# Layer 1 of a two-layer decoder trunk: issue order held from its first stage, and the main products reordered to keys, values, receptance, gate

## Chip, cores and metric

The kernel runs on one NeuronCore of a Trainium2 chip. The metric is the device time of one execution in microseconds (us); the kernel before takes 2486.07 us, the median of three runs (2485.39 to 2491.46). A difference of 0.3% is 7.5 us.

## The reference

A sequence of 512 tokens with 2048 features passes two layers, all in float32. Layer 0 is a forgetting attention; the change does not touch its work. Layer 1 is RWKV-7 time mixing (here without the constants):

```python
h = rms_norm(x, norm_w[1]) * (1 + scale) + shift
xx = pad(h[:, :-1]) - h                       # the token before, minus this one
xr, xw, xk, xv, xa, xg = (h + xx * mu[i] for i in range(6))
r, k, v, z = xr @ w_in[0], xk @ w_in[1], xv @ w_in[2], xg @ w_in[3]
w_log = -softplus(-(w0 + tanh(xw @ w1) @ w2)) - 0.5;  decay = exp(-exp(w_log))
v = v + (v_first - v) * sigmoid(v0 + (xv @ v1) @ v2)
a = sigmoid(a0 + (xa @ a1) @ a2)
kk = normalised(k * k_k);  k = k * (1 + (a - 1) * k_a)
for t: S = S * w_t + (S @ a_t) b_t + v_t k_t;  y_t = S @ r_t      # per head of 64, a = -kk, b = kk * a
y = group_norm(y) * lnx_w + lnx_b + sum(r * k * r_k) * v
x = x + gate * ((y * silu(z)) @ w_out)
```

So the receptance r, the key k, the value v and the gate z are four products of 2048 x 2048, each from its own mix of h with the token before, and the output is a fifth. The scan over the tokens is computed in chunks of 64 tokens.

## The kernel before

Features lie on the 128 partitions, in KT = 16 tiles of 128 x 512 tokens. A product of float32 accuracy is three matmuls in float32r: weight and operand are each split into `hi` (a copy on ScalarE, ACT) and `lo` (a subtraction on VectorE, DVE), and `mm3` adds hi x hi, lo-weight x hi and hi x lo-operand in one PSUM bank. One output tile of a main product is 16 x 3 = 48 matmuls of 512 columns.

Layer 1 has these stretches.

- **First stage.** One loop over the 16 feature tiles k. It forms the normalised tile `xn` (DVE), the hidden tile `hp` (ACT, stored to `h1d`), the difference to the token before `d`, the key's mix `m` and its split, the split of one 128 x 768 slice of the key weight (`wst1`), and 18 matmuls into six banks: the first six key tiles. It also forms the mixes of the receptance and of the gate (ACT multiplies, GpSimd (POOL) adds) and stores them to `mxd[1]` and `mxd[2]`. In this loop the three compute engines are not held to program order; the scheduler of the framework may put one tile's work ahead of another's.
- **Main products.** `backbone` runs over a list of output tiles: ten remaining keys, 16 receptances, 16 values, 16 gates, 16 outputs. Their operands come from `mixed`, which loads a stored mix and splits it, when a tile of the operand before is spent. Two PSUM banks (`pj`) take turns; tile i waits in the plan until the work behind tile i - 2 has let go of its bank (`freed`). At the boundary between two products two tiles are interleaved.
- **Side work.** While `backbone` writes out its matmuls, a planner (`Flow`) interleaves generators by a planned clock `fl.t`, which counts the matmuls written so far: first `lora_k` (three small products, and the value's mix, stored to `mxd[0]`), then `lora_up`, then `keys` (one per head pair, 9.8 planned us apart) with `invert` and `inverse` (a triangular inverse, most of it on POOL, then through TensorE), then, when all 16 inverses are stored (`qd`), the pool `rk` is opened and `stage` and `chain` run the recurrence: 16 chains, each begun at least 12 hops of 2.15 planned us after the one before.
- **Order.** From `backbone` on, PE (TensorE), DVE and ACT each issue in exactly the order in which the program was written (`e.on = True`). SP (SyncE) issues nearly all transfers, on one queue.

`values` needs the pool `rk` for its buffers, which before is open only after the inverses; `stage` needs `rd` (a receptance tile stored) and `vd` (a value tile stored and transposed). `gated` waits for `yd` (a chain's output stored).

Of the kernel before, what the change touches and what calls it, by code (L numbers as in the profile page):

```python
# [9 lines left out]
F = mybir.dt.float32  # L10
# [7 lines left out]
P = 128  # L18
# [111 lines left out]
def body(ctx, tc, a, out, dbg=None, stop=0):  # L130
# [49 lines left out]
    bsc = cp.tile([P, 2, KT], F, name="bsc")  # L180
    for l in range(2):
        pool.tensor_scalar(bsc[:, l, :], vecs[:, V_BM + 3 * l + 1, :], 1.0, None, op0=OP.add)
    mraw = cp.tile([P, 6, 2 * KT], F, name="mraw")
    shift = cp.tile([P, 2, KT], F, name="shift")
    scale = cp.tile([P, 2, KT], F, name="scale")
    gate = cp.tile([P, 2, KT], F, name="gate")
# [6 lines left out]
    pool.memset(floor, 2.0 ** 26 * 1e-24 / DH)  # L193
    oka = cp.tile([P, KT], F, name="oka")
    pool.tensor_scalar(oka, vecs[:, V_KA, :], -1.0, 1.0, op0=OP.mult, op1=OP.add)
    lnb = cp.tile([P, 1], F, name="lnb")
    pool.memset(lnb, 10.0 * LN2)
    center = cp.tile([P, P], F, name="center")
# [65 lines left out]
    def mod_unit(mp, cb, l, part, t):  # L264
        for h in range(2):
            s = slice(h * D // 2, (h + 1) * D // 2)
            w = mp.tile([P, D // 2], F, tag="wm", name="wm", bufs=3)
            sp.dma_start(w, a["wmodT"][l, part * KT + t][:, s])
            yield 4.5
            dve.tensor_tensor_reduce(out=w, in0=w, in1=cb[:, s], scale=1.0, scalar=0.0,  # L270
                                     op0=OP.mult, op1=OP.add,
                                     accum_out=mraw[:, 3 * l + part, 2 * t + h:2 * t + h + 1])
            mdone.add((l, part, t, h))
        m0, m1 = (mraw[:, 3 * l + part, 2 * t + h:2 * t + h + 1] for h in range(2))
        b = vecs[:, V_BM + 3 * l + part, t:t + 1]
        if part == 1:
            b = bsc[:, l, t:t + 1]
        o = (shift, scale, gate)[part][:, l, t:t + 1]
        pool.tensor_scalar(o, m0, m1, b, op0=OP.add, op1=OP.add)
        if part == 1:  # L280
            pool.tensor_scalar(o, o, vecs[:, V_NW + l, t:t + 1], 1.0, op0=OP.mult, op1=OP.mult)
# [105 lines left out]
    with ExitStack() as s0:  # L387
# [7 lines left out]
        with tc.tile_pool(name="st0", bufs=2, reuse_waits="tile") as q:  # L395
# [201 lines left out]
        def until(i):  # L597
            while i is not None and i not in ends:
                yield 0.2
# [313 lines left out]
        backbone(fl, tiles, at, ready, ends, {n - 2, n} if 1 else ())  # L913
        fl.drain()
        gst.close()
        for e in (pe, dve, act):
            e.on = False
        ss = bank("ss")
        for i, t in enumerate(acc):
            pe.matmul(ss, onesD, t, start=i == 0, stop=i == 1)  # L920
# [8 lines left out]
        A = []  # L929
        ks = [bank(t) for t in ("pj", "pj", "x", "x", "S", "S")]  # L930
        with tc.tile_pool(name="st1", bufs=2, reuse_waits="tile") as q:
            for k in range(KT):
                xp = q.tile([P, T + 1], F, tag="xn", name="xn")
                xn = xp[:, 1:]
                pool.tensor_scalar(xp[:, 0:1], shift[:, 1, k:k + 1], -1.0, 1.0, op0=OP.mult,
                                   op1=OP.mult)
                dve.scalar_tensor_tensor(out=xn, in0=x1[k], scalar=scale[:, 1, k:k + 1],
                                         in1=rstd1, op0=OP.mult, op1=OP.mult)
                hp = q.tile([P, T + 1], F, tag="hp", name="hp")
                pool.memset(hp[:, 0:1], 0.0)  # L940
                act.activation(hp[:, 1:], xn, AF.Identity, bias=shift[:, 1, k:k + 1])
                sp.dma_start(h1d[k], hp)
                w = wload(a["wst1"][k:k + 1].rearrange("k p n -> p k n"), 1, NS1, "s", q)
                A.append(new_act(k))
                d = q.tile([P, T], F, tag="d", name="d")
                dve.tensor_tensor(out=d, in0=xp[:, 0:T], in1=xn, op=OP.subtract)
                m = q.tile([P, T], F, tag="m", name="m")
                dve.scalar_tensor_tensor(out=m, in0=d, scalar=vecs[:, V_MU + 2, k:k + 1],
                                         in1=hp[:, 1:], op0=OP.mult, op1=OP.add)
                split(A[k][0], A[k][1], m)  # L950
                for i, n in ((1, 0), (2, 5)):
                    m = q.tile([P, T], F, tag=f"m{n}", name="m")
                    act.activation(m, d, AF.Copy, scale=vecs[:, V_MU + n, k:k + 1])
                    pool.tensor_tensor(out=m, in0=m, in1=hp[:, 1:], op=OP.add)
                    sp.dma_start(mxd[i, k], m)
                for i, o in enumerate(ks):
                    mm3(o, w, 0, A[k], k == 0, k == KT - 1, i * P, (i + 1) * P)

# [8 lines left out]
    fl = Flow()  # L967
    NK = KT - len(ks)
    mq = ctx.enter_context(tc.tile_pool(name="mq", bufs=2, reuse_waits="tile"))
    pools = ExitStack()  # L970
    ctx.callback(pools.close)
    q = pools.enter_context(tc.tile_pool(name="kq", bufs=2, reuse_waits="tile"))
# [65 lines left out]
    def mixing(i, to, old):  # L1038
        for k in range(KT):
            while (i, k) not in premixed:  # L1040
                yield 0.2
            yield from take("m")
            fl.start(fl.t + 2, mixed(i, to, old, k, load(mq, mxd[i, k], "hp", bufs=NHP)))
            yield 0.1

    premixed = {(i, k) for i in (1, 2) for k in range(KT)}

    def keep(j, o):
        t = mq.tile([P, T], F, tag="z", name="kt")
# [110 lines left out]


    def values(j, o, e):
        while not vqs:
            yield 0.2
        vq = vqs[0]
        yield from take("vf")
        yield from take("sv")
        sv = load(vq, svd[j], "sv", bufs=1)
        vv = load(vq, vfT[j], "vf", bufs=2)
        yield from until(e)  # L1170
        dve.tensor_tensor(out=vv, in0=vv, in1=o, op=OP.subtract)
        yield 0.7
        dve.tensor_tensor(out=vv, in0=vv, in1=sv, op=OP.mult)
        free["sv"] += 1
        yield 0.7
        dve.tensor_tensor(out=vv, in0=vv, in1=o, op=OP.add)
        yield 3
        sp.dma_start(vvd[j], vv)
        n = yield from need("S")
        tr = bank("S")  # L1180
        for i in range(4):
            pe.transpose(tr[:, i * P:(i + 1) * P], vv[:, i * P:(i + 1) * P], ident)
        yield 1
# [6 lines left out]
        vd.add(j)  # L1190


    md = set()
# [438 lines left out]
    def side(q):  # L1632
# [35 lines left out]
        for j in range(KT):  # L1668
            if "v" in dbg:
                print("keys", j, fl.t, len(ends))  # L1670
            fl.start(fl.t, keys(kp, j))
            yield KEY
        while len(qd) < KT:
            yield 0.2
        yield 3
        pools.close()
        rk = pools.enter_context(tc.tile_pool(name="rk", bufs=1, reuse_waits="tile"))
        vqs.append(rk)
        for i in range(4):
            QP.append([rk.tile([P, HC, C], F, name=f"QP{i}{h}") for h in range(2)])  # L1680
            GP.append([rk.tile([P, HC, C], F, name=f"GP{i}{h}") for h in range(2)])
# [19 lines left out]
            fl.start(fl.t, chain(rk, j))  # L1701
            yield 0.1

    vqs = []
    fl.start(0, side(q))
    Av, Ar, Az, G = [], [], [], []
    ready = {(id(A), k) for k in range(KT)}
    at = {}
    tiles = [(a["wk1"][j], A, kept, j) for j in range(KT - NK, KT)]
    tiles += [(a["wr"][j], Ar, recept, j) for j in range(KT)]  # L1710
    tiles += [(a["wv1"][j], Av, values, j) for j in range(KT)]
    tiles += [(a["wz1"][j], Az, gated, j) for j in range(KT)]
    tiles += [(a["wo1"][j], G, output, j) for j in range(KT)]
    for e in (pe, dve, act):
# [1 line left out]
    pe.clock = fl  # L1716
    freed.clear()
    n0, n1, n2, n3 = NK, NK + KT, NK + 2 * KT, NK + 3 * KT
    for n, task in ((n0, mixing(1, Ar, A)), (n1, mixing(0, Av, Ar)), (n2, mixing(2, Az, Av)),
                    (n3, gathering())):  # L1720
        at[n - 2, 0] = [task]
    backbone(fl, tiles, at, ready, ends, {n - i for n in (n0, n1, n2, n3) for i in (0, 2)}, 14)
# [22 lines left out]
```

## Time and profile before

| what | number |
|---|---|
| time, median of three runs | 2486.07 us |
| the profiled execution | 2484.87 us, its span 2483.2 us |
| mean granted TensorE clock | 0.979 |
| PE busy | 2342.1 us (94%) |
| DVE, ACT, POOL busy | 1658.1, 1242.7, 756.2 us |
| DMA, mean | 192 GB/s, 476.06 MB |

Matmuls overlap, so PE's busy time is the time in which at least one runs. A timeline row gives start, duration, engine, line, operation, output<-inputs. A window row gives its length, the busy time of PE, of the weight loads, of DVE, ACT and POOL with instruction counts, the granted clock, the mean share of the 16 DMA engines that was busy, and GB/s. All instructions are issued through one helper, so they carry one line number, and tiles are told apart by name.

### The profile page before, as it was taken

The numbers are of one execution on the slowest core, as the hardware profiler recorded it, in microseconds if no ns is written. First come the engines' busy times: TensorE is split into PE (matmuls) and PEld (weight loads), VectorE is DVE, ScalarE is ACT, GpSimd is POOL, SyncE is SP. The second block draws the span as 40 slices with busy tenths as digits, with TensorE's granted clock in tenths as the row PEclk, the third lists the DMA queues.
The fourth block names the chain that finished last, engine by engine and source line by source line (L and its number), as shares of the span: only waits on it lengthen the run. The fifth ranks groups of instructions, "written<-read, shape, count | busy, mean of one in ns | idle before, by whom it ended". The sixth has DMA issues, their size and how long they took to land. (4 is left out here: it accounts for less than half of the span.)

```text
span 2483.2 us, 39895 instructions
## 1 busy us (share of the span) xinstructions
PE 2342.1 (94%) x13626; PEld 1812.4 (73%) x13626; DVE 1658.1 (67%) x3114; ACT 1242.7 (50%) x2281; POOL 756.2 (30%) x1199
## 2 busy tenths in 40 slices
PE   7998999999999999987999998887999999999999
PEld 4786677787777888865766776765777767777787
DVE  7878787888887553349796666572577876776332
ACT  3426655555556552226447676642344545555321
POOL 0003424433332200117340248720434444441000
PEclk8999999999999999999999999998999999999999
DMA  8856566666664275436657886776656656554453
GB/s 315 314 210 208 179 198 215 208 211 202 211 202 153 94 234 173 146 117 215 193 168 254 264 253 213 215 209 188 199 156 174 194 155 180 158 146 154 142 148 98
DMA packets 339260, 476.06 MB, mean 192 GB/s; under 512 B 146288, under 2 KB 156656, under 8 KB 335216
## 3 DMA queue, kind: packets, MB, share of 16 engines
q1 hardware_dynamic: 337392, 470.88, 60.5%
q0 software_dynamic: 1664, 2.63, 0.3%
q8 instruction: 108, 1.77, 0.3%
q14 instruction: 96, 0.79, 0.1%
HBM read 377.42 MB, written 95.95 MB: 191 GB/s over the span
## 5 line engine op out<-in xcount | busy, mean ns | idle before, releaser
L88 PE MATMUL pj<-hi,whi 128*128 128x512 f32 x2416 | 990.4, 410 | 16.8 <-ACT hi L88 10.3
L88 PE MATMUL pj<-hi,wlo 128*128 128x512 f32 x2416 | 954.7, 395 | 17.8 <-DVE wlo L88 17.8
L88 PE MATMUL pj<-lo,whi 128*128 128x512 f32 x2416 | 956.4, 396 | 2.3 <-DVE lo L88 2.3
L88 DVE TENSOR_TENSOR wlo<-raw,whi 128x512 fp32r<-128x512 f32 (+2 forms) x628 | 477.8, 768 | 278.5 <-ACT whi L88 276.0
L88 ACT ACTIVATE whi<-raw 128x512 fp32r<-128x512 f32 (+2 forms) x628 | 393.6, 634 | 412.6 <-PE pj L88 232.7
L88 PEld LDWEIGHTS pj<-hi,whi 128*128 128x128 f32 x2416 | 458.5, 190 | 122.7 <-ACT hi L88 11.6
L88 PEld LDWEIGHTS pj<-hi,wlo 128*128 128x128 f32 x2416 | 459.1, 190 | 108.3 <-DVE wlo L88 22.9
L88 PEld LDWEIGHTS pj<-lo,whi 128*128 128x128 f32 x2416 | 457.2, 189 | 104.1 <-DVE lo L88 3.4
L88 POOL TENSOR_SCALAR SV<-SV,dec 64x64 f32<-64x64 f32 x224 | 91.8, 410 | 221.7 <-DVE SV L88 207.3
L88 DVE CUSTOM_DVE_ANT_0 wm<-wm,cb 128x1024 f32<-128x1024 f32 x128 | 157.8, 1233 | 0.3
L88 ACT ACTIVATE pr<-Sm,mx 128x128 f32<-128x128 f32 (+3 forms) x128 | 71.5, 559 | 87.9 <-POOL mx L88 87.7
L88 POOL TENSOR_SCALAR mx<-mx 128x1 f32<-128x1 f32 x128 | 64.9, 507 | 158.2 <-DVE mx L88 110.0
L88 POOL TENSOR_SCALAR pr<-pr,rc 128x128 f32<-128x128 f32 (+3 forms) x128 | 96.0, 750 | 28.2 <-DVE rc L88 20.2
L88 DVE COPY SV<-x 64x64 f32<-64x64 f32 x256 | 56.6, 221 | 63.3 <-PE x L88 56.2
L88 DVE CUSTOM_DVE_ANT_0 Sm<-S,cmask 128x128 f32<-128x128 f32 (+3 forms) x128 | 62.1, 485 | 35.5 <-PE S L88 34.8
L88 POOL TENSOR_TENSOR lt<-lane 128x30 f32<-128x30 f32 (+14 forms) x90 | 61.3, 682 | 64.6 <-DMA lane<-mld 57.8
L88 DVE TENSOR_TENSOR SV<-SV,x 64x64 f32<-64x64 f32 x224 | 48.9, 218 | 37.9 <-PE x L88 32.3
L88 POOL TENSOR_TENSOR acc<-acc,sq 128x512 f32<-128x512 f32 x14 | 18.1, 1296 | 161.4 <-ACT sq L88 126.1
L88 POOL TENSOR_TENSOR lane<-lane,lt 128x30 f32<-128x30 f32 (+14 forms) x90 | 63.9, 710 | 7.1
L88 PE MATMUL S<-k,q 128*128 128x128 f32 (+7 forms) x256 | 62.7, 326 | 0.0
L88 PE MATMUL tr<-ident,pr 128*128 128x128 f32 x320 | 56.8, 275 | 4.6 <-ACT pT L88 1.6
L88 POOL TENSOR_TENSOR bk<-bk,eI 128x512 f32<-128x512 f32 x32 | 36.8, 1148 | 78.6 <-PE S L88 43.7
(321 smaller groups left out, 3439.6 us busy)
## 6 DMA issues: line engine op xcount, KB each, us to landing
wm<-in_wmodT SPq DMA_DIRECT2D x132, 512.0 KB, 4.3
raw<-in_wz SPq DMA_DIRECT2D x128, 256.0 KB, 3.8
raw<-in_wo SPq DMA_DIRECT2D x128, 256.0 KB, 3.5
raw<-in_wv SPq DMA_DIRECT2D x124, 256.0 KB, 3.7
wm<-in_wmodT SPq DMA_DIRECT2D x30, 1024.0 KB, 6.8
raw<-in_wk SPq DMA_DIRECT2D x96, 256.0 KB, 3.8
raw<-in_wr SPq DMA_DIRECT2D x64, 256.0 KB, 4.3
raw<-in_wq SPq DMA_DIRECT2D x56, 256.0 KB, 3.6
```

The lines of the kernel that those rows point to most:

```text
L88: self.last = f(*a, **k)
```

## The change

Layer 1's first stage is written in a fixed order with PE, DVE and ACT held to it, and forms the key's mix alone, as `hp * mu + h * (1 - mu)`. Its hidden tile is made two tiles ahead, the weight split two ahead, the key's mix one ahead. The mixes for receptance and gate are made by a new generator `mixrz`, one beside each `keys`: it loads `h1d[k]`, forms the difference and the two mixes on DVE, and stores both. Values are the second product and receptance the third; `values` gets a buffer pool of its own, starts when its sigmoid is stored, and lets go of the bank after its third DVE operation. The pool `rk` is opened when all inverses, all values and all mixes are stored. The index of a small tile (`mraw`) is shifted, and one constant tile `omk` is added.

```diff
-        for e in (pe, dve, act):
-            e.on = False
...
-            for k in range(KT):
-                xp = q.tile([P, T + 1], F, tag="xn", name="xn")
-                xn = xp[:, 1:]
-                pool.tensor_scalar(xp[:, 0:1], shift[:, 1, k:k + 1], -1.0, 1.0, op0=OP.mult,
-                                   op1=OP.mult)
...
+            def hidden(k):
+                xn = q.tile([P, T], F, tag="xn", name="xn")
                 dve.scalar_tensor_tensor(out=xn, in0=x1[k], scalar=scale[:, 1, k:k + 1],
                                          in1=rstd1, op0=OP.mult, op1=OP.mult)
...
                 act.activation(hp[:, 1:], xn, AF.Identity, bias=shift[:, 1, k:k + 1])
                 sp.dma_start(h1d[k], hp)
-                w = wload(a["wst1"][k:k + 1].rearrange("k p n -> p k n"), 1, NS1, "s", q)
+            def mix(k):
+                g = gms[k] = q.tile([P, T], F, tag="g", name="g", bufs=3)
+                act.activation(g, hps[k][:, 1:], AF.Copy, scale=omk[:, k:k + 1])
+                m = mks[k] = q.tile([P, T], F, tag="m", name="m")
+                dve.scalar_tensor_tensor(out=m, in0=hps.pop(k)[:, 0:T],
+                                         scalar=vecs[:, V_MU + 2, k:k + 1], in1=gms.pop(k),
+                                         op0=OP.mult, op1=OP.add)
                 A.append(new_act(k))
+                act_hi(A[k][0], m)
-                d = q.tile([P, T], F, tag="d", name="d")
-                dve.tensor_tensor(out=d, in0=xp[:, 0:T], in1=xn, op=OP.subtract)
...
-                split(A[k][0], A[k][1], m)
-                for i, n in ((1, 0), (2, 5)):
-                    m = q.tile([P, T], F, tag=f"m{n}", name="m")
-                    act.activation(m, d, AF.Copy, scale=vecs[:, V_MU + n, k:k + 1])
-                    pool.tensor_tensor(out=m, in0=m, in1=hp[:, 1:], op=OP.add)
-                    sp.dma_start(mxd[i, k], m)
...
+            for k in range(KT):
+                if k + 2 < KT:
+                    hidden(k + 2)
+                if k + 1 < KT:
+                    mix(k + 1)
+                w_load(k + 3)
+                w_hi(k + 2)
+                w_lo(k + 2)
+                if k + 1 < KT:
+                    low(k + 1)
+                w = ws.pop(k)
                 for i, o in enumerate(ks):
                     mm3(o, w, 0, A[k], k == 0, k == KT - 1, i * P, (i + 1) * P)
...
     def values(j, o, e):
-        while not vqs:
+        while (j, 2) not in ups:
             yield 0.2
-        vq = vqs[0]
...
         dve.tensor_tensor(out=vv, in0=vv, in1=o, op=OP.add)
+        freed.add(e)
...
+    def mixrz(q, k):
+        yield from take("m")
+        hp = load(mq, h1d[k], "hp", (P, T + 1), bufs=NHP)
+        yield 5
+        d = q.tile([P, T], F, tag="md", name="d", bufs=1)
+        dve.tensor_tensor(out=d, in0=hp[:, 0:T], in1=hp[:, 1:], op=OP.subtract)
+        yield 1
+        for i, n in ((1, 0), (2, 5)):
+            m = q.tile([P, T], F, tag="mm", name="m", bufs=2)
+            dve.scalar_tensor_tensor(out=m, in0=d, scalar=vecs[:, V_MU + n, k:k + 1],
+                                     in1=hp[:, 1:], op0=OP.mult, op1=OP.add)
+            yield 1.5
+            sp.dma_start(mxd[i, k], m)
+            premixed.add((i, k))
+        free["m"] += 1
...
             fl.start(fl.t, keys(kp, j))
+            fl.start(fl.t + 5, mixrz(kp, j))
             yield KEY
-        while len(qd) < KT:
+        while len(qd) < KT or len(vd) < KT or len(premixed) < 3 * KT:
             yield 0.2
...
     tiles = [(a["wk1"][j], A, kept, j) for j in range(KT - NK, KT)]
+    tiles += [(a["wv1"][j], Av, values, j) for j in range(KT)]
     tiles += [(a["wr"][j], Ar, recept, j) for j in range(KT)]
-    tiles += [(a["wv1"][j], Av, values, j) for j in range(KT)]
     tiles += [(a["wz1"][j], Az, gated, j) for j in range(KT)]
     tiles += [(a["wo1"][j], G, output, j) for j in range(KT)]
```

More of the change, by code (lines that the diff above doesn't have):

```diff
@@ L182, in body @@
         pool.tensor_scalar(bsc[:, l, :], vecs[:, V_BM + 3 * l + 1, :], 1.0, None, op0=OP.add)
-    mraw = cp.tile([P, 6, 2 * KT], F, name="mraw")
+    mraw = cp.tile([P, 4, 2 * KT], F, name="mraw")
     shift = cp.tile([P, 2, KT], F, name="shift")
@@ L195, in body @@
     pool.tensor_scalar(oka, vecs[:, V_KA, :], -1.0, 1.0, op0=OP.mult, op1=OP.add)
+    omk = cp.tile([P, KT], F, name="omk")
+    pool.tensor_scalar(omk, vecs[:, V_MU + 2, :], -1.0, 1.0, op0=OP.mult, op1=OP.add)
     lnb = cp.tile([P, 1], F, name="lnb")
@@ L271, in mod_unit @@
                                      op0=OP.mult, op1=OP.add,
-                                     accum_out=mraw[:, 3 * l + part, 2 * t + h:2 * t + h + 1])
+                                     accum_out=mraw[:, 3 * l + part - 2, 2 * t + h:2 * t + h + 1])
             mdone.add((l, part, t, h))
-        m0, m1 = (mraw[:, 3 * l + part, 2 * t + h:2 * t + h + 1] for h in range(2))
+        m0, m1 = (mraw[:, 3 * l + part - 2, 2 * t + h:2 * t + h + 1] for h in range(2))
         b = vecs[:, V_BM + 3 * l + part, t:t + 1]
@@ L931, in body, with w_load, w_hi @@
         with tc.tile_pool(name="st1", bufs=2, reuse_waits="tile") as q:
-            for k in range(KT):
-                xp = q.tile([P, T + 1], F, tag="xn", name="xn")
-                xn = xp[:, 1:]
-                pool.tensor_scalar(xp[:, 0:1], shift[:, 1, k:k + 1], -1.0, 1.0, op0=OP.mult,
-                                   op1=OP.mult)
+            rws, ws, xns, hps, gms, mks = ({} for _ in range(6))
+            def w_load(k):
+                if k < KT:
+                    rws[k] = q.tile([P, 1, NS1], F, tag="raws", name="raw", bufs=3)
+                    sp.dma_start(rws[k], a["wst1"][k:k + 1].rearrange("k p n -> p k n"))
+            def w_hi(k):
+                if k < KT:
+                    hi = q.tile([P, 1, NS1], R, tag="whis", name="whi", bufs=3)
+                    act_hi(hi, rws[k])
+                    ws[k] = hi, q.tile([P, 1, NS1], R, tag="wlos", name="wlo", bufs=3)
+            def hidden(k):
+                xn = q.tile([P, T], F, tag="xn", name="xn")
                 dve.scalar_tensor_tensor(out=xn, in0=x1[k], scalar=scale[:, 1, k:k + 1],
                                          in1=rstd1, op0=OP.mult, op1=OP.mult)
-                hp = q.tile([P, T + 1], F, tag="hp", name="hp")
+                hp = hps[k] = q.tile([P, T + 1], F, tag="hp", name="hp", bufs=3)
                 pool.memset(hp[:, 0:1], 0.0)
@@ L942, in body, with w_lo, low @@
                 sp.dma_start(h1d[k], hp)
-                w = wload(a["wst1"][k:k + 1].rearrange("k p n -> p k n"), 1, NS1, "s", q)
-                A.append(new_act(k))
-                d = q.tile([P, T], F, tag="d", name="d")
-                dve.tensor_tensor(out=d, in0=xp[:, 0:T], in1=xn, op=OP.subtract)
-                m = q.tile([P, T], F, tag="m", name="m")
-                dve.scalar_tensor_tensor(out=m, in0=d, scalar=vecs[:, V_MU + 2, k:k + 1],
-                                         in1=hp[:, 1:], op0=OP.mult, op1=OP.add)
-                split(A[k][0], A[k][1], m)
-                for i, n in ((1, 0), (2, 5)):
-                    m = q.tile([P, T], F, tag=f"m{n}", name="m")
-                    act.activation(m, d, AF.Copy, scale=vecs[:, V_MU + n, k:k + 1])
-                    pool.tensor_tensor(out=m, in0=m, in1=hp[:, 1:], op=OP.add)
-                    sp.dma_start(mxd[i, k], m)
+            def mix(k):
[5 more added lines that the diff above has]
+                                         op0=OP.mult, op1=OP.add)
+                A.append(new_act(k))
+                act_hi(A[k][0], m)
+            def w_lo(k):
+                if k < KT:
+                    dve.tensor_tensor(out=ws[k][1], in0=rws.pop(k), in1=ws[k][0],
+                                      op=OP.subtract)
+            def low(k):
+                dve.tensor_tensor(out=A[k][1], in0=mks.pop(k), in1=A[k][0], op=OP.subtract)
+            for k in range(3):
+                w_load(k)
+            w_hi(0)
+            w_lo(0)
+            hidden(0)
+            hidden(1)
+            mix(0)
+            w_hi(1)
+            w_lo(1)
+            low(0)
+            for k in range(KT):
[9 more added lines that the diff above has]
+                w = ws.pop(k)
                 for i, o in enumerate(ks):
@@ L969, in body @@
     mq = ctx.enter_context(tc.tile_pool(name="mq", bufs=2, reuse_waits="tile"))
+    vst = ExitStack()
+    ctx.callback(vst.close)
+    vq = vst.enter_context(tc.tile_pool(name="vq", bufs=2, reuse_waits="tile"))
     pools = ExitStack()
@@ L1044, in mixing @@
             yield 0.1
-    premixed = {(i, k) for i in (1, 2) for k in range(KT)}
+    premixed = set()
     def keep(j, o):
@@ L1190, in values @@
         vd.add(j)
+    def mixrz(q, k):
+        yield from take("m")
+        hp = load(mq, h1d[k], "hp", (P, T + 1), bufs=NHP)
+        yield 5
+        d = q.tile([P, T], F, tag="md", name="d", bufs=1)
[9 more added lines that the diff above has]
+        free["m"] += 1
     md = set()
@@ L1676, in side @@
         pools.close()
+        vst.close()
         rk = pools.enter_context(tc.tile_pool(name="rk", bufs=1, reuse_waits="tile"))
-        vqs.append(rk)
         for i in range(4):
@@ L1702, in side @@
             yield 0.1
-    vqs = []
     fl.start(0, side(q))
@@ L1718, in body @@
     n0, n1, n2, n3 = NK, NK + KT, NK + 2 * KT, NK + 3 * KT
-    for n, task in ((n0, mixing(1, Ar, A)), (n1, mixing(0, Av, Ar)), (n2, mixing(2, Az, Av)),
+    for n, task in ((n0, mixing(0, Av, A)), (n1, mixing(1, Ar, Av)), (n2, mixing(2, Az, Ar)),
                     (n3, gathering())):
```

## The prediction, made before the changed kernel was run

> **What bounds the kernel now.** I read the page's totals first, then a table of stretches of layer 1, then the waits of PE in three of them.
>
> ```profile
> span 2483.2 us, 39895 instructions
> PE 2342.1 (94%) x13626; PEld 1812.4 (73%) x13626; DVE 1658.1 (67%) x3114; ACT 1242.7 (50%) x2281; POOL 756.2 (30%) x1199
> ```
>
> PE has work running in 94% of the span, and the change removes no matmul from it. So all that can be won is time in which PE stands, and all that can be lost is more of it. The table says where PE stands in layer 1.
>
> ```profile
> core 0: us, PE busy (x) PEld busy (x) DVE busy (x) ACT busy (x) POOL busy (x), PEclk, DMA share, GB/s
> 0.00:50.00 50.00, 34.42 (x115) 23.08 (x116) 34.09 (x44) 21.67 (x35) 5.01 (x24) 0.90 0.88 331
> ...
> 1114.00:1207.00 93.00, 75.94 (x289) 57.25 (x290) 79.34 (x77) 51.55 (x79) 59.07 (x60) 0.92 0.67 213
> 1372.00:1588.00 216.00, 190.95 (x1193) 148.20 (x1191) 136.48 (x177) 151.99 (x279) 119.22 (x162) 0.96 0.78 238
> 1698.00:1713.00 15.00, 2.24 (x9) 1.84 (x10) 3.98 (x7) 1.81 (x5) 4.61 (x19) 0.63 0.81 248
> 1713.00:1752.00 39.00, 33.37 (x155) 26.19 (x155) 16.85 (x28) 11.11 (x21) 9.84 (x19) 0.88 0.70 191
> 1752.00:2300.00 548.00, 537.24 (x4570) 395.40 (x4570) 384.40 (x1005) 276.79 (x479) 210.80 (x426) 0.99 0.59 167
> ```
>
> The reader is to see five things. The first stage (1114 to 1207) leaves PE idle for 17 us. The keys stretch (1372 to 1588) leaves it idle for 25 us while the DMA engines are busy for 0.78 of the time. At the opening of the recurrence's pool (1698 to 1752) it is idle for 18 us and partly at a low granted clock. The chains (1752 to 2300) leave 11 us of 548. After them come the output tiles, PE alone. The waits name the causes: in the first stage DVE's `wlo`, at the pool's opening the value tile `vf`, in the chains again `vf`, and at their end the operand of the first output tiles.
>
> ```profile
> PE pj L88 <- DVE wlo L88: 14.7, 9, 3.1
> PE S L88 <- DVE vf L88: 13.1, 2, 11.3
> PE S L88 <- DVE vf L88: 2.9, 1, 2.9
> PE pj L88 <- ACT hi L88: 2.2, 1, 2.2
> ```
>
> The last row matters for the sum: PE waits for the last chain's result before output tiles 14 and 15 of the operand can be used, so the end follows the chains. The chains are written out by planned hops, and their stretch keeps its length; **the end moves as the first chain's start moves.**
>
> **Part 1, the first stage.** Rows of it, in order of time:
>
> ```profile
> 1108.74 0.69 DVE L88 SCALAR_TENSOR_TENSOR rs<-rs1u,rs 128x512 f32<-128x512 f32 x1
> ...
> 1114.05 0.79 PE L88 MATMUL pj<-hi,whi 128*128 128x512 f32 x1 [8.18 <-ACT hi L88]
> ...
> 1140.89 1.87 DVE L88 TENSOR_TENSOR wlo<-raw,whi 128x768 fp32r<-128x768 f32 x1
> ...
> 1176.82 0.74 DVE L88 SCALAR_TENSOR_TENSOR xn<-x,scale,rs 128x512 f32<-128x512 f32 x1
> ...
> 1178.08 0.74 DVE L88 SCALAR_TENSOR_TENSOR m<-d,vecs,hp 128x512 f32<-128x512 f32 x1
> 1178.74 0.95 DVE L88 TENSOR_TENSOR wlo<-raw,whi 128x768 fp32r<-128x768 f32 x1
> 1178.85 0.63 ACT L88 ACTIVATE hi<-m 128x512 fp32r<-128x512 f32 x1 [0.55 <-DVE m L88]
> 1179.39 0.71 ACT L88 ACTIVATE m<-d,vecs 128x512 f32<-128x512 f32 x1
> 1179.61 0.68 DVE L88 TENSOR_TENSOR lo<-m,hi 128x512 fp32r<-128x512 f32 x1
> 1180.00 0.71 ACT L88 ACTIVATE hp<-xn,shift 128x512 f32<-128x512 f32 x1
> 1180.21 0.68 DVE L88 TENSOR_TENSOR d<-xn 128x512 f32<-128x512 f32 x1
> 1193.91 0.84 ACT L88 ACTIVATE whi<-raw 128x768 fp32r<-128x768 f32 x1 [0.49 <-DMA raw<-in_wst]
> ...
> 1206.48 0.39 PE L88 MATMUL S<-hi,wlo 128*128 128x512 f32 x1
> 1206.71 0.40 PE L88 MATMUL S<-lo,whi 128*128 128x512 f32 x1
> ```
>
> Now: from 1114.05 to 1206.94 (the last start plus the pitch of 0.23) is 92.9 us, 5.81 per tile. PE alone needs 288 x 0.23 = 66. What sets the pace is DVE, with operations stretched beside POOL's additions: the same `wlo` takes 1.87 at 1140.89 and 0.95 at 1178.74.
>
> The change takes out of each tile the DVE difference, two ACT multiplies, two POOL adds and two stores; it adds one ACT multiply (`g`). That leaves DVE 0.74 + 0.74 + 0.95 + 0.68 = 3.1 us and ACT 0.71 + 0.71 + 0.63 + 0.84 = 2.9, each under PE's 18 x 0.23 = 4.1. But both queues are now held to the written order, and that order is a ring. DVE: xn(k+2), m(k+1), wlo(k+2), lo(k+1). ACT: hp(k+2), g(k+1), hi(k+1), whi(k+2). hp waits for xn; g stands behind hp; m waits for g; hi waits for m; whi stands behind hi; wlo waits for whi; lo stands behind wlo, and the next xn behind lo. One turn, with the pitch where two follow on one engine: xn 0.74 + hp 0.61 (1179.39 to 1180.00) + g 0.71 + m 0.74 + hi 0.54 (1178.85 to 1179.39) + whi 0.84 + wlo 0.87 (1178.74 to 1179.61) + lo 0.60 (1179.61 to 1180.21) + four crossings of 0.03 to 0.08 = **5.8 us**. The two engines hardly overlap.
>
> Start: from 1108.74 DVE does rs 0.62, wlo(0) 0.87, xn(0) 0.74, ACT hp(0), hp(1), g(0) (0.61 + 0.61 + 0.71), DVE m(0) 0.74, ACT hi(0) 0.63: first matmul at about 1114.4, lo(0) at 1116.8. Then 14 turns to lo(14) at 1198.0, a short turn to lo(15) at 1200.0, and PE ends 34 matmuls after 1198.0, at 1205.9. **-1 us**; between +6 (whole durations instead of pitches, 6.2 a turn) and -26 (92.9 - 66, rival C). PE's waits turn from `wlo` to `lo`. The small products after the stage start from its end and are DVE's anyway: nothing. `omk` and the `mraw` index: nothing, at the kernel's start beside transfers.
>
> **Part 2, the keys stretch.** What moves into it:
>
> ```profile
> L88 SPq DMA_DIRECT2D ip<-ipd x16: 320/431/1173, 1372.1 to 1574.9; - x16
> ...
> raw<-in_wr SPq DMA_DIRECT2D x48, 256.0 KB, 4.5
> ...
> rTd<-r SPq DMA_DIRECT2D x10, 256.0 KB, 3.8
> ...
> L88 DVE TENSOR_TENSOR wlo<-raw,whi 128x512 fp32r<-128x512 f32 x53 | 41.7, 790 | 41.7 <-ACT whi L88 41.7
> ...
> L88 DVE TENSOR_TENSOR vf<-vf,pj x32: 677/687/690, 1706.3 to 1995.3; 128x512 f32<-128x512 f32 x32
> ...
> L88 PE MATMUL S<-ident,vf x64: 270/273/476, 1709.0 to 1996.8; 128*128 128x128 f32 x64
> ```
>
> Transfers: `mixrz` issues one load and two stores per key, 47 of 48 inside the stretch; a value tile has two loads and two stores where a receptance tile has one store, with ten such tiles 43 - 10 = 33. That is 80 transfers of 256 KB on SP's queue. In this stretch 238 GB/s took a share of 0.78, so a full share moves 305 GB/s, and 262144 bytes cost 0.86 us of it: 80 x 0.86 = 69 us. The stretch needs 0.78 x 216 = 168 us of the DMA engines now and 237 then, of 216. At a full share that is +21. The longest busy stretch of this profile runs at 0.88 (0 to 50): 237 / 0.88 = 269, +53. At the other end 0: stores are not waited for, and backlog may drain after the keys. I take the middle, **+27**, a share of 0.975, since the demand stands nearer the upper half than idle. Below nothing I exclude: nothing but a 0.6 us copy per tile leaves.
>
> DVE gains 47 x 0.79 and 30 x 0.79, 61 us on 136.5: 91% of 216. Behind a waiting mix or value operation stands `wlo`, for which PE waits, and behind a store that waits for DVE stand SP's weight loads. I count that in the same 27, as the same stretching. PE gets the 64 transposes earlier: they are in the planned clock and push the tiles, not the keys.
>
> **Part 3, the opening of the pool.**
>
> ```profile
> L88 SPq DMA_DIRECT2D qtd<-qt x16: 319/388/728, 1545.0 to 1699.3; - x16
> ...
> L88 PE MATMUL x<-SV,L x512: 222/222/367, 1753.8 to 2297.0; 128*64 128x64 f32 x171
> ```
>
> Now 54.5 us pass from the last inverse stored (1699.3) to the first chain (1753.8), with PE stopped since no value tile can leave its bank. After the change receptance tiles run here and leave at once, so that 13.1 us wait goes. What is late next is the first receptance tile: the transposes (64 x 0.213 planned) put PE 1.3 tiles further back, and the tile, interleaved with its neighbour, is stored about one tile of 11 us (48 x 0.23) after the inverses. From there the yields of `stage` to the first chain add to 28 planned us; the chain stretch runs 548 us for 15 x 25.8 + 23 x 2.15 = 436 planned, a factor 1.25: 35 us. 11 + 35 = 46 against 54.5: **-8**; between -18 (all idle time of 1698 to 1752) and +6 (factor 1.5 in a burst of stage loads on SP).
>
> **Part 4, chains and end.** Values leave the chains: the 2.9 us wait goes, **-3** (0 to -6). DVE and DMA relief there buys nothing, PE being busy 98%. The last chain's wait stays.
>
> **Sum.** -1 + 27 - 8 - 3 = +15 on the profiled 2484.87 (span 2483.2 and 1.7 around it; the median of the runs, 2486.07, lies 1.2 above): **2500 us**.
>
> **Rivals.** *A, the forecast*: the keys stretch grows by 15 to 40; 2485 to 2515. *B, the transfers are hidden, faster*: the stretch grows by under 4.5 us, its point of decision, and the stall at the pool is a clean gain: -1 + 0 - 8 - 3, 2473. For it: single slices carry more than 305 GB/s.
>
> ```profile
> 1365.00:1370.00 5.00, 5.00 (x24) 4.08 (x23) 2.56 (x3) 4.01 (x8) 3.18 (x11) 1.00 1.00 358
> 1500.00:1505.00 5.00, 5.00 (x24) 4.09 (x23) 4.77 (x7) 3.85 (x8) 4.45 (x8) 1.00 1.01 387
> ```
>
> The stretch would need 238 + 80 x 0.262 MB / 216 us = 335 GB/s. Against it: these slices are at a full share, and no 50 us stretch passes 331. The Trainium skill (HBM Reference, section Specifications (TRN2)) states that a core streaming alone measures about 425 GB/s; by that rule 335 fits and the time is B's. The trace does not bear it out for these mixed transfers, which fill a share of 0.78 with 238.
>
> *C, the ring overlaps*: DVE and ACT run ahead and PE sets the first stage: 2500 - 25 = 2475. For it: each engine has 3 us of work for PE's 4.1. Against it: the written order, unless it is not what the queues hold. *D, the keys stretch is worse*: DVE at 91% in order holds up `wlo` and the keys' chain of steps together, at +53: 2526. For it: DVE's 41.7 us of waits before `wlo` are dependences that no other work fills.
>
> **Chances.** A 0.52, B 0.20, C 0.10, D 0.18. With 0.3% as what a measurement can tell (7.5 us: 2477 and 2492): faster 0.15 from B, 0.07 from C, 0.04 from A's low end, 0.26; the same 0.05 + 0.03 + 0.10, 0.18; slower 0.56. The range 2465 to 2530 takes in B, C and D with a few us about each.
>
> **What would show it.** First stage: 92 us again, DVE and ACT each about half idle in it, PE waiting for `lo`; at 66 to 75 us C holds. Keys stretch: `ip` loads 14.5 to 16 us apart (now 13.5), a DMA share over 0.9 and longer landings than 4.5 us for the weights; 13.5 or less would be B. Pool: no wait of PE for `vf` after the last inverse, the first chain about 46 us after it. End: the chains' stretch 545 us long. The forecast is wrong if the stretch's transfers spread or if the ring is not a ring.

## The result, and the profile after

The kernel after takes 2510.64 us (median of four runs, 2504.21 to 2513.45) against 2488.33 for the kernel before on the same chip: a ratio of 1.0086, with a 95% interval from 1.0061 to 1.011. It is slower by 0.86%. The profiled execution took 2510.57 us, its span is 25.7 us longer than before's, and the totals hardly move:

```profile
span 2508.9 us, 39817 instructions
PE 2346.4 (94%) x13626; PEld 1816.1 (72%) x13626; DVE 1654.8 (66%) x3146; ACT 1239.0 (49%) x2269; POOL 708.6 (28%) x1152
```

What moved is seen by cutting the span at the same events. Three tiles give the marks: the load of each key's `ip`, the store of each inverse (`qtd`), and the first and last chain step. A row gives the shortest, median and longest duration in ns, then the first and the last start in us.

```profile
L88 SPq DMA_DIRECT2D ip<-ipd x16: 320/453/1623, 1375.1 to 1600.8; - x16
...
L88 SPq DMA_DIRECT2D qtd<-qt x16: 319/372/505, 1568.4 to 1736.1; - x16
...
L88 PE MATMUL x<-SV,L x512: 221/222/272, 1787.3 to 2327.0; 128*64 128x64 f32 x171
```

| stretch | before, us | after, us | change | forecast |
|---|---|---|---|---|
| start to the end of layer 0 | 1103.0 | 1100.6 | -2.4 | 0 |
| to the first matmul of the first stage | 11.0 | 11.6 | +0.6 | in the next |
| first stage | 92.7 | 94.1 | +1.4 | -1 |
| to the first `ip` | 165.4 | 168.8 | +3.4 | 0 |
| first `ip` to the last inverse stored | 327.2 | 361.0 | +33.8 | +27 |
| to the first chain | 54.5 | 51.2 | -3.3 | -8 |
| chains | 543.2 | 539.7 | -3.5 | -3 |
| to the end | 186.2 | 181.9 | -4.3 | 0 |

Table of stretches of the kernel after, the columns as before (length, busy PE, weight loads, DVE, ACT, POOL, granted clock, DMA share, GB/s): the first stage, the keys, the opening of the pool, the chains.

```profile
1112.00:1207.00 95.00, 74.64 (x289) 55.01 (x290) 47.96 (x65) 42.98 (x66) 3.76 (x15) 0.95 0.36 117
...
1375.00:1601.00 226.00, 192.88 (x1160) 148.74 (x1159) 180.13 (x238) 147.03 (x268) 121.17 (x155) 0.92 0.92 292
...
1736.00:1787.00 51.00, 45.38 (x202) 35.10 (x202) 18.29 (x29) 15.75 (x31) 14.26 (x32) 0.90 0.73 186
...
1787.00:2331.00 544.00, 537.76 (x4570) 396.40 (x4569) 363.36 (x974) 284.16 (x485) 209.36 (x424) 1.00 0.54 153
```

In the first stage DVE has 48 us of work where it had 79, POOL 4 where it had 59, and PE still stands for 20 us. The keys stretch has its DMA engines busy for 0.92 of the time. The opening of the pool has lost its stall, and the chains leave 6 us.

The first stage is a ring, as the next rows show (timeline of DVE and of ACT in the kernel after, one turn):

```profile
1125.56 0.68 DVE L88 TENSOR_TENSOR lo<-m,hi 128x512 fp32r<-128x512 f32 x1
1126.16 0.74 DVE L88 SCALAR_TENSOR_TENSOR xn<-x,scale,rs 128x512 f32<-128x512 f32 x1
...
1126.99 0.72 ACT L88 ACTIVATE hp<-xn,shift 128x512 f32<-128x512 f32 x1 [2.34 <-issue]
...
1127.62 0.71 ACT L88 ACTIVATE g<-hp,omk 128x512 f32<-128x512 f32 x1
...
1128.43 0.75 DVE L88 SCALAR_TENSOR_TENSOR m<-hp,vecs,g 128x512 f32<-128x512 f32 x1 [1.52 <-ACT g L88]
...
1129.21 0.63 ACT L88 ACTIVATE hi<-m 128x512 fp32r<-128x512 f32 x1 [0.89 <-DVE m L88]
...
1129.75 0.83 ACT L88 ACTIVATE whi<-raw 128x768 fp32r<-128x768 f32 x1
...
1130.61 0.96 DVE L88 TENSOR_TENSOR wlo<-raw,whi 128x768 fp32r<-128x768 f32 x1 [1.43 <-ACT whi L88]
1131.49 0.68 DVE L88 TENSOR_TENSOR lo<-m,hi 128x512 fp32r<-128x512 f32 x1
1132.09 0.75 DVE L88 SCALAR_TENSOR_TENSOR xn<-x,scale,rs 128x512 f32<-128x512 f32 x1
```

One engine works while the other waits, and a turn takes 1131.49 - 1125.56 = 5.93 us. PE's waits there, by engine and tile (us in total, times, longest):

```profile
PE pj L88 <- DVE lo L88: 20.1, 13, 1.6
```

### The profile page after: what moved, and what is told of

Same layout as the page of the kernel before. It is cut to its first block, busy times and chain, and to the rows that moved or that the text cites. A ratio compares the mean times of both kernels' runs of the same rounds, so it can differ in the third digit from the quotient of the medians.

```text
span 2508.9 us, 39817 instructions
## 1 busy us (share of the span) xinstructions
PE 2346.4 (94%) x13626; PEld 1816.1 (72%) x13626; DVE 1654.8 (66%) x3146; ACT 1239.0 (49%) x2269; POOL 708.6 (28%) x1152
## 4 chain that ended last, share of the span: by engine, by line
PE 31%; DVE 9%; DMA 7%; ACT 4%; issue 3%; SPq 2%; ACTq 0%; DVEq 0%
PE pj L88 23%; PE S L88 4%; PE x L88 3%; DVE m L88 2%; DVE wlo L88 2%; SPq L88 2%; DMA raw<-in_wv 1%; PE y L88 1%; DMA kt<-kTd 1%; ACT whi L88 1%; DMA raw<-in_wr 1%; DVE kk L88 1%; ACT sig L88 1%; DVE mlo L88 1%; DVE vf L88 1%
## 5 line engine op out<-in xcount | busy, mean ns | idle before, releaser
L88 PEld LDWEIGHTS pj<-lo,whi 128*128 128x128 f32 x2416 | 460.0, 190 | 127.8 <-DVE lo L88 26.9
L88 POOL TENSOR_TENSOR lt<-lane 128x30 f32<-128x30 f32 (+14 forms) x90 | 66.8, 742 | 73.1 <-DMA lane<-mld 66.2
L88 DVE SCALAR_TENSOR_TENSOR m<-d,vecs,hp 128x512 f32<-128x512 f32 x80 | 69.2, 876 | 0.4
```

Source lines behind the costliest of these rows:

```text
L88: self.last = f(*a, **k)
```

## The experiments

Times are compared by the ratio to the kernel before, with its 95% interval; stretches are those of the table above. The kernel before, timed again beside them, stands at 2487.36 us for e1 to e4, 2486.39 for e5 to e8 and 2486.3 for e9 to e12. A profile is of one execution, up to 10 us from its kernel's median: e4's is its shortest (2501.28), e1's its longest (2487.6). So stretches of two kernels compare to a few us only. Layer 0 is the same in the kernel after and in e1 to e6, and ends between 1096.6 and 1103.7 us in their profiles.

**The ring: e1 and e2.** e1 keeps the operations of the first stage and writes them in another order, so that what an operation needs was written one step earlier (`xn_of` and `m_of` are DVE's, `g_of` and `hp_of` ACT's):

```diff
-                if k + 2 < KT:
-                    hidden(k + 2)
+                m_of(k + 1)
+                xn_of(k + 3)
+                g_of(k + 2)
                 if k + 1 < KT:
-                    mix(k + 1)
+                    act_hi(A[k + 1][0], mks[k + 1])
                 w_load(k + 3)
                 w_hi(k + 2)
-                w_lo(k + 2)
+                hp_of(k + 3)
                 if k + 1 < KT:
                     low(k + 1)
+                w_lo(k + 2)
```

> The changed kernel with only the writing order of the first stage altered: the hidden tile is made three tiles ahead instead of two, and each of its steps is written so that what an engine waits for was begun one turn earlier (DVE: m, xn, lo, wlo; ACT: g, hi, whi, hp); the same instructions. Theory (the held order is a ring of 5.8 us a tile): the first stage falls from 94 us to 66-72 us, PE-bound, and nothing behind it changes, so 2510 - 24 = 2484 to 2490 us. Rival (DVE or the weight transfers set the stage): it stays at 90 us or more and the time within 5 us of 2510.

e2 changes no line of the stage, and lets the scheduler order it as before the change:

```diff
+        for e in (pe, dve, act):
+            e.on = False
```

> The changed kernel with the hold on PE, DVE and ACT taken off in the first stage alone, the same writing. Theory (the hold makes the ring): the framework's scheduler lets DVE and ACT run ahead, the stage takes 66-78 us instead of 94, the time 2488 to 2498. Rival (the dependences between the operations, not the hold, make the ring): 90 us or more, 2505 to 2515.

e1 took 2479.19 us, ratio 0.9969 (0.9953 to 0.9984), and e2 2479.9, ratio 0.9961 (0.9947 to 0.9975), 5 and 8 us below their ranges. The first stage takes 67.9 us in e1 and 66.7 in e2, against 94.1, near PE's own 66. The stage of e1 as a window, and PE's only wait in it:

```profile
1110.00:1180.00 70.00, 66.02 (x279) 54.40 (x280) 51.55 (x70) 47.27 (x69) 3.78 (x14) 0.93 0.59 171
```

```profile
PE pj L88 <- ACT hi L88: 7.4, 1, 7.4
```

That is the start of the stage; no wait for `lo` is left, with the same operations. With the engines held, the written order alone keeps the stage at 94 us. Undoing it is worth 26 us in the stage and 1.17% (1.0086 against 0.9969), 29 us, of the time; where the other 3 lie is not known. Both kernels are faster than the kernel before, but e9 below shows what that comparison mixes in.

**The mixes in the keys stretch: e3, e4, e5.** Each is the kernel after with a part of `mixrz` left out. e3 leaves out its load and its two stores (the mixes are formed from a constant tile, and receptance and gate then read the value's mix):

```diff
-        hp = load(mq, h1d[k], "hp", (P, T + 1), bufs=NHP)
+        hp = hpc[0]
...
-            sp.dma_start(mxd[i, k], m)
```

> The changed kernel in which the mixes beside the keys keep their three DVE operations but neither load nor store; they work on a constant tile, and receptance and gate read the value's mix (the result is that of other operands). It takes 48 of the 80 added transfers out of the keys stretch. Theory (the DMA engines' share stretches the keys): the DMA share there falls from 0.92 to about 0.8, the keys come every 13.8 us instead of 15.0, and the time falls by 12 to 20 to 2490-2498. Rival (DVE in order does): the keys stay at 14.6 us or more and the time at 2504-2512.

e4 leaves out its three DVE operations and stores the unmixed tile in their place:

```diff
-        dve.tensor_tensor(out=d, in0=hp[:, 0:T], in1=hp[:, 1:], op=OP.subtract)
...
-            sp.dma_start(mxd[i, k], m)
+            sp.dma_start(mxd[i, k], hp[:, 1:])
```

> The changed kernel in which the mixes beside the keys keep their load and both stores (the hidden tile itself is stored, so receptance and gate are those of the unmixed hidden tile) but not their three DVE operations. Theory (transfers): DVE falls from 190 to about 150 us busy in the stretch, but the keys stay at 14.5 us or more and the time within 6 us of 2510. Rival (DVE): the keys come every 13.8 us and the time falls by 12 to 20.

e5 leaves out both (receptance and gate are then products of the unmixed hidden state):

```diff
-        hp = load(mq, h1d[k], "hp", (P, T + 1), bufs=NHP)
...
+        yield 9
+        premixed.update(((1, k), (2, k)))
```

> The changed kernel without the mixes beside the keys: neither transfers nor DVE operations (receptance and gate read the hidden tile itself). Theory (the DMA engines' share stretches the keys, DVE's operations do not): no different from the kernel without the mixes' transfers, 2497 within 5 us, with 345-350 us from the first load of a key's decay to the last inverse. Rival (transfers and DVE operations each do part): 6 us or more below it.

| kernel | time, us | ratio | first `ip` to last inverse |
|---|---|---|---|
| after | 2510.64 | 1.0086 (1.0061 to 1.011) | 361.0 |
| e4, no DVE operations | 2511.06 | 1.0085 (1.0055 to 1.0115) | 356.8 |
| e3, no transfers | 2497.01 | 1.0044 (1.0029 to 1.0059) | 349.3 |
| e5, neither | 2491.2 | 1.0022 (1.001 to 1.0034) | 344.0 |

The transfers cost 0.42%, 10 us, by e3; the DVE operations alone nothing that e4's interval of 0.3% to either side can tell; both together 0.64%, 16 us, by e5. With the transfers gone the DVE operations do count: from e3 to e5 the time falls by another 0.22%, 5 to 6 us, and the stretch by 5.3 us. e5 was expected within 5 us of 2497, or by the rival 6 us or more below; at 5.8 us below it meets neither. The windows of the keys stretch of e3 and of e4, beside that of the kernel after above:

```profile
1375.00:1601.00 226.00, 192.06 (x1202) 148.48 (x1203) 192.56 (x253) 152.06 (x277) 136.78 (x169) 0.93 0.84 256
```

```profile
1375.00:1601.00 226.00, 186.36 (x1141) 142.79 (x1139) 147.15 (x197) 146.84 (x269) 118.20 (x163) 0.94 0.92 293
```

DVE at 193 us of 226 with the DMA share at 0.84 is the faster stretch; DVE at 147 with the share at 0.92 is the slow one. The `ip` loads come every 14.2 us in e3 and 13.9 in e5, against 15.0 in e4 and 15.05 in the kernel after. The mixes strain the DMA engines first and DVE second.

**The order of the products: e6.** e5 with the old order again, receptance ahead of the values, and the values waiting for the pool `rk` as before; the first stage stays that of the change. e5's emptied `mixrz`, which still held a load buffer for 9 planned us beside each key, goes too.

```diff
-    tiles += [(a["wv1"][j], Av, values, j) for j in range(KT)]
     tiles += [(a["wr"][j], Ar, recept, j) for j in range(KT)]
+    tiles += [(a["wv1"][j], Av, values, j) for j in range(KT)]
```

> The same without the mixes, and the product order of before besides (keys, receptance, values, gate; values wait for the recurrence's pool). What is left of the change is the first stage in its held order. Theory (the values' 33 added transfers are the rest of the keys' growth): from the first decay load to the last inverse 325-333 us instead of 347, and the stall at the pool's opening comes back, 54-56 us from the last inverse to the first chain; the time 2482-2492, that of before, since the held first stage lasts as long as the one of before. Rival (the rest comes from elsewhere): 340 us or more, 2495 or more.

2486.45 us, ratio 0.9997 (0.9987 to 1.0007), as expected: the new order costs 0.25%, 6 us, against e5. By stretches it costs 344.0 - 323.4 = 20.6 us up to the last inverse and gives back 5.9 at the pool, 3.1 in the chains and 3.0 at the end. Where the 20.6 lie is read from windows cut at the marks (length, busy PE with its count of matmuls, clock, DMA share, GB/s; keys to inverses, pool, chains, end), first of e6, then of e5:

```profile
1377.10:1700.50 323.40, 291.65 (x2294) 0.95 0.76 226
1700.50:1755.60 55.10, 36.07 (x172) 0.81 0.73 202
1755.60:2297.90 542.30, 532.89 (x4541) 0.99 0.59 167
2297.90:2482.50 184.60, 178.51 (x794) 1.00 0.42 130
```

```profile
1375.60:1719.60 344.00, 301.22 (x2331) 0.93 0.81 245
1719.60:1768.80 49.20, 42.12 (x204) 0.97 0.72 187
1768.80:2308.00 539.20, 533.69 (x4543) 1.00 0.55 153
2308.00:2489.60 181.60, 165.33 (x725) 0.96 0.40 121
```

PE is busy 9.6 us longer before the last inverse and idle 11.0 us longer (42.8 against 31.8). The busy part is the values' 64 transposes, which all move to this side. In the kernel after they stand here:

```profile
L88 PE MATMUL S<-ident,vf x64: 270/273/421, 1443.6 to 1723.9; 128*128 128x128 f32 x64
```

At 0.27 us each they are 17.5 us. The count of matmuls rises by only 37, so 27 of output tiles, 6 us, were pushed out of the stretch; some 10 us of the transposes fell on the path of the keys. Of the idle part 8.6 us are waits for value tiles, which e6 does not have there: for 4.8 us a transpose waits for `vf`, for 3.8 an output tile waits for the bank that the value operation reads. PE issues in written order, so the keys' matmuls behind stand too. The kernel after has 13 us of the same waits before its last inverse (PE's waits from 1375 to 1614, then from 1614 to 1790):

```profile
PE S L88 <- DVE vf L88: 5.9, 4, 2.7
...
PE S L88 <- DVE vf L88: 3.7, 2, 2.1
PE pj L88 <- DVE vf L88: 3.4, 1, 3.4
```

The last rows of the two tables show what becomes of the tiles pushed out and of those that ran at the pool and in the chains: 69 fewer matmuls are left for the end, yet the end is only 3 us shorter, since PE then stands there for 16 us instead of 6, waiting for the last chain. The kernel after shows the same (PE's waits from 2300 to 2350, where before had 2.2):

```profile
PE pj L88 <- ACT hi L88: 9.1, 1, 9.1
```

**The mixes at their use: e7 and e8.** With the ring-free first stage of e1, receptance and gate mix where they are used: `mixed` loads `h1d` instead of a stored mix and does one ACT multiply and one DVE operation. `mixrz` goes, with its 48 transfers; 1 - mu stands in two new constant tiles. e7 has the new product order, e8 the old one (and one load buffer `hp` fewer).

```diff
+    om = {}
+    for i, n in ((1, 0), (2, 5)):
+        om[i] = cp.tile([P, KT], F, name=f"om{i}")
...
+            act.activation(m, hp[:, 1:], AF.Copy, scale=om[i][:, k:k + 1])
+            dve.scalar_tensor_tensor(out=m, in0=hp[:, 0:T],
+                                     scalar=vecs[:, V_MU + (0, 0, 5)[i], k:k + 1], in1=m,
+                                     op0=OP.mult, op1=OP.add)
```

> The whole computation, from the kernel with the first stage's ring broken: the mixes of receptance and gate are formed where their operand is needed (the hidden tile is loaded instead of a stored mix, one ACT and one DVE operation more for each), so the 48 transfers beside the keys are gone and nothing takes their place. New product order. Theory: 2479 less the 13.6 us that the transfers cost, plus 0 to 8 us where 16 mixes fall together at the change of product: 2466 to 2474. Rival (the operations at the change of product hold up PE as much): 2476 or more.

> The whole computation as in the run before it in this list, with the product order of the kernel before and four instead of five load buffers (space). Theory (the new order costs more in the keys than it gains at the pool, about 10 us): 2456 to 2468, the fastest. Rival (the order is worth its gain once the transfers are gone): as the run before it or slower.

Both missed by over 35 us: 2509.68, ratio 1.009 (1.0073 to 1.0107), and 2514.34, ratio 1.0108 (1.0092 to 1.0123). The first stage was 68.9 us in both, near e1's 67.9. The loss showed where nothing had been edited: layer 0 ended at 1114.8 in e7 against 1100.6 in the kernel after. In a stretch of layer 0 in which PE never stands, the number of matmuls differs between kernels. The same window of before, of after, and of e7 (the second pair of numbers is PE's busy time and its matmuls):

```profile
1000.00:1080.00 80.00, 80.00 (x351) 65.65 (x350) 29.56 (x36) 21.21 (x36) 9.06 (x7) 1.00 0.44 143
```

```profile
1000.00:1080.00 80.00, 80.00 (x355) 66.25 (x354) 29.87 (x37) 20.68 (x36) 9.04 (x7) 1.00 0.44 142
```

```profile
1000.00:1080.00 80.00, 80.00 (x346) 64.87 (x345) 28.86 (x36) 20.58 (x35) 9.06 (x7) 1.00 0.42 140
```

The full clock is granted in all three, the instructions are the same, and the mean pitch from one matmul's start to the next is 229, 227 and 232 ns. What differs are the constant tiles allocated ahead of everything else: per partition, `mraw` is 768 bytes before, `mraw` and `omk` 576 bytes after, and with e7's two more tiles it is 704. So later tiles lie at other addresses.

**Only the place: e9, e10, e11.** e9 is the kernel before with tile sizes that put the later constants, and what follows them, where they lie after:

```diff
-    mraw = cp.tile([P, 6, 2 * KT], F, name="mraw")
+    mraw = cp.tile([P, 4, 2 * KT], F, name="mraw")
...
+    spare = cp.tile([P, KT], F, name="spare")
+    pool.memset(spare, 0.0)
```

> The kernel before, with nothing changed but the sizes of its constant tiles: mraw has four rows instead of six and a 64-byte spare tile is added, so that every later tile lies where it lies in the kernel after. If the place of the tiles sets the pitch of the matmuls, the dense output tiles go from 229 to about 226.7 ns per matmul, and the time is 3 to 10 us under before, with the loss spread over output tiles and chains and none of it in the keys stretch. If the place does nothing, pitch and time stay as before, and the shorter chain stretch of after comes from the values that left it.

e10 is the kernel after with the place of before:

```diff
+    spare = cp.tile([P, 3 * KT], F, name="spare")
+    pool.memset(spare, 0.0)
```

> The kernel after with a spare constant tile of 192 bytes, so that later tiles lie as they lie in before. Place theory: pitch 229 ns, chain stretch back to 542 to 545 us, 3 to 10 us slower than after: 2513 to 2520. Rival (the values' leaving is what shortened the chains): as after, 2510, chain stretch 539.7.

e11 is e7 with its two tiles in columns that are dead after layer 0:

```diff
-        om[i] = cp.tile([P, KT], F, name=f"om{i}")
+        om = {1: scale[:, 0, :], 2: shift[:, 0, :]}
```

> e7 again (new product order, the receptance's and gate's mixes made where they are used, from the hidden state, with no transfers of their own), but with its two tiles of 1 - mu put into columns that are dead after layer 0, so that the other tiles lie as in after. Place theory: pitch 226.7 instead of 232 ns, and 2466 to 2476. Rival: e7 was slow because the mixes at the change of product hold up PE; then the pitch improves and the time stays at 2495 or more.

The same window of e9, e10 and e11:

```profile
1000.00:1080.00 80.00, 80.00 (x355) 66.27 (x354) 31.10 (x39) 22.88 (x39) 10.34 (x8) 1.00 0.45 145
```

```profile
1000.00:1080.00 80.00, 80.00 (x351) 65.63 (x351) 29.25 (x36) 21.21 (x36) 9.05 (x7) 1.00 0.45 146
```

```profile
1000.00:1080.00 80.00, 80.00 (x355) 66.24 (x354) 29.22 (x36) 21.15 (x36) 9.04 (x7) 1.00 0.44 144
```

The count follows the place in all three. e9 took 2478.08 us, ratio 0.9966 (0.9955 to 0.9978): 8 us gained with no work changed. e10 took 2516.94, ratio 1.0122 (1.0106 to 1.0137), 6 us more than after. e11 took 2485.0, ratio 0.9997 (0.9987 to 1.0007), 25 us less than e7. So the place explains most of e7's miss. It also takes the gain from e1 and e2: at their own place of the constants the kernel before, as e9, stands at 0.9966, beside e1's 0.9969 and e2's 0.9961. They show what the ring costs the kernel after, not a gain over the old first stage. The rest of e7's miss is e11's own: its keys stretch (first `ip` 1346.4, last inverse 1693.2) is 17 us shorter than e1's, but its chains take 555.3 us instead of 539.9, and it lies between the two expectations. Which step of the mixing lengthens the chains was not separated.

The chains hardly follow the place, against the expectations of e9 and e10: 542.7 in e9 and 543.2 before, 541.0 in e10 and 539.7 after.

**The best version: e12.** The old order of the products, all three mixes in the first stage, and the first stage without a ring:

```diff
+            def others(k):
+                for i, n in ((1, 0), (2, 5)):
+                    if k < KT:
+                        g = q.tile([P, T], F, tag=f"g{n}", name=f"g{n}")
+                        act.activation(g, oth[k][:, 1:], AF.Copy, scale=om[i][:, k:k + 1])
+                        og[i, k] = g
+                    if 0 <= k - 1 < KT:
+                        g = og.pop((i, k - 1))
+                        dve.scalar_tensor_tensor(out=g, in0=oth[k - 1][:, 0:T],
+                                                 scalar=vecs[:, V_MU + n, k - 1:k], in1=g,
+                                                 op0=OP.mult, op1=OP.add)
+                        sp.dma_start(mxd[i, k - 1], g)
```

> The old product order (receptance, keys, values, gate as in before) and all three mixes in the first stage as in before, but with the first stage written so that no ring forms, the mixes as one ACT multiply and one DVE operation each and none on POOL, tiles placed as in after. If the ring was what held the first stage, it takes 68 to 75 us instead of 92.7, the keys stretch stays at about 325 and the time is 2456 to 2468. Rival: with three mixes DVE (3 x 0.74 + 0.74 + 0.95 + 0.68 = 4.6 us a tile against PE's 4.1) and ACT (about 4.3) are the bound and the stage takes 80 or more: 2470 to 2480.

2472.57 us, ratio 0.9939 (0.9925 to 0.9952), the fastest of all, and 0.27%, some 6 us, below e9 at the same place of the constants. The stage takes 74.3 us, as expected; the total misses its range by 5 us and falls into the rival's, whose stage of 80 us or more it does not have. What follows the stage takes back part of its gain: from 1187 the small products need 111 us against 101 before.

```profile
PE pj L88 <- ACT kt L88: 7.5, 1, 7.5
```

PE waits for the first key tiles' copy out of PSUM, which on ACT stands behind a weight split that waits for its load:

```profile
1192.95 0.63 ACT L88 ACTIVATE whi<-raw 128x512 fp32r<-128x512 f32 x1 [4.55 <-DMA raw<-in_wk]
1193.49 1.07 ACT L88 ACTIVATE kt<-pj 128x512 f32<-128x512 f32 x2
```

## Why the prediction was right, and where its steps were not

The direction and the mechanism that decides it, rival A, held: a longer keys stretch outweighs what the pool's opening gives. The forecast was +15 us, the spans show +25.7. That the two lie so near is partly luck, since terms missed on both sides and one that was put at nothing took 6 to 8 us off.

**First stage, -1, measured +1.4.** The ring was there and e1 shows that it is the bound: taken away, the stage falls to PE's 66 to 68 us, as rival C had it for a ring that overlaps. The turn was sized 5.8 us and takes 5.93 to 6.02. With the same place of the constants, e6 (ring, two mixes left out of the kernel) takes 2486.45 us and e9 (the old stage with its three mixes) 2478.08. By their profiles 4.9 of these 8 us lie in the stage (96.5 against 91.6; the same stage took 94.1 in the kernel after). Another 4.8 lie in layer 0, in which neither differs from the other, so they are the scatter of single executions. Freed of two thirds of its mixes, the new stage is 2.5 to 5 us longer than the old one. The small products behind it, put at "nothing", took 3.4 us longer; no run separates why.

**Keys, +27, measured +33.8, by two causes, one of them misjudged.** The transfers were rightly feared. The stretch reached a share of 0.92 at 292 GB/s, between the 0.88 that gave the forecast its upper end and the 0.975 of its middle; the `ip` loads came 15.05 us apart, in the forecast's 14.5 to 16, and the weights landed later than 4.5 us after their issue. Between 1375 and 1614 stand 74 added transfers, where the sum had 80, and the DMA engines were busy for 0.92 of 239 us, 220, where it had 237. The weights' landing:

```profile
raw<-in_wv SPq DMA_DIRECT2D x43, 256.0 KB, 5.1
```

Rival B was the same transfers hidden. By the rule of the Trainium skill (HBM Reference, section Specifications (TRN2)) about 425 GB/s would have let 335 through. No keys stretch here bears that out: at 0.92 of the engines the mixed transfers made 292.

But `mixrz` accounts for only 17.0 of the stretch's growth (361.0 against e5's 344.0), 11.7 of them by its transfers (e3's 349.3) and 5.3 by its DVE operations. The new order accounts for 20.6 (e5 against e6's 323.4), and e6 itself is 3.8 us shorter than before. Most of the order's part is a step that failed: the transposes "push the tiles, not the keys". They pushed the tiles by 27 matmuls, 6 us of their 17.5, and the keys by some 10 us, with 8.6 us of waits for value tiles beside them. So the +27, priced by 80 transfers, came near the total partly by luck. What the values' transfers and their DVE operations cost in it was not tried alone.

**Opening of the pool, -8, measured -3.3.** The wait for `vf` is gone here and PE is idle for 5.6 us of 51 instead of 18 of 54, as said. Most of it has moved, though: PE waited 16.0 us for `vf` before, at the pool and in the chains, and waits 13 now, in the keys. Both terms of the 46 us were wrong, in opposite directions. The first receptance tile was stored 3.7 us after the last inverse (1739.8), not 11, and the steps from there to the first chain took 47.5 us, not 35: a factor of 1.7 on the 28 planned, past the 1.5 of the range's upper end. ACT waited 26.9 us for weights (`raw<-in_wr`) in this stretch; whether that stretched the steps is not shown. PE worked through them, 202 matmuls in 51 us where it had done 164 in 54.

**Chains, -3, measured -3.5**, 539.7 against the forecast's 545 for the stretch. At equal place it is 541.0 against 543.2 and 539.7 against 542.7, so -2 to -3 belong to the values that left.

**End, 0, measured -4.3.** Fewer output tiles are left for it, 725 matmuls instead of 794, and PE loses part of the gain in the longer wait for the last chain, 9.1 us instead of 2.2.

**The index of `mraw` and `omk`, "nothing", measured -6 to -8.** This is the term that failed outright: not the operations, the addresses. It shows in the pitch of the dense stretches. How many us each stretch took of it single profiles do not tell: layer 0 and the end are 5.6 and 1.7 us shorter in e9 than before, 3.8 and 2.4 longer in e10 than after, but layer 0 varies by up to 7 us between profiles at one place. Without it the change costs 1.22% (e10 to before) or 1.20% (after to e9), 30 us, twice the forecast. The steps between e9 and the kernel after, all at one place, add up to it by construction: the first stage and what else parts e6 from e9, 8; the order, 5 to 6 (e6 to e5); the mixes, 16 to 19 (e5 to after).

## What to carry to other kernels

When two engines are held to program order, write out one turn as a chain through both queues before costing the operations: removing two thirds of the mixes changed nothing while the chain was 5.9 us a tile, and moving each operation one step ahead, with no work changed, gave 26 us. Work moved ahead of a critical sequence counts on every engine that the sequence uses, PE's small transposes too, and the keys stretch, at a DMA share of 0.78, had no room for the mixes' transfers. Compare kernels only at equal placement of their tiles: an added or shrunk constant can be worth more than the edit under study, as between e1 and the kernel before, and a stretch that nothing edited is where it shows.

## What was not expected of the hardware

The pitch of identical matmuls (128 x 128 by 128 x 512, fp32r, full granted clock, PE never idle) was 227, 229 or 232 ns, by a shift of all later SBUF tiles by 64 to 192 bytes per partition. It moved the time by 0.3% (e9 to before) and by 0.9% (e7 to e11). Which of the tiles has to lie where, and why, no run here tells apart.
